# Attention in a hybrid DeltaNet block: the low-part products of the value step issued apart from the high-part products

## The chip, the core and the metric

The kernel runs on one core of one Trainium2 chip. The metric is the device time of the whole program in microseconds (us). The core has five engines that run side by side, each through its own list of instructions in order: TensorE (PE in the profile, with its weight loads as PEld), VectorE (DVE), ScalarE (ACT), GpSimd (POOL) and SyncE (SP), which issues the transfers.

## What is computed

One layer of a streaming encoder on 2048 tokens of 1024 channels. The normalised input goes through one wide projection; that feeds a gated delta rule (4 heads of 128) and a stick-breaking attention (8 heads of 64); both results are gated, projected, merged and added to the input. The part that matters here is the attention:

```python
def _stick_breaking(q, k, v):
    ...
    for blk in range(s // SB_BLOCK):
        ...
        z = jnp.einsum('bhqd,bhkd->bhqk', q[:, :, q0:end], k[:, :, :end]) * scale
        ...
        log_keep = jnp.where(mask, jax.nn.log_sigmoid(-z), 0.0)
        rest = lax.cumsum(log_keep, axis=3, reverse=True) - log_keep
        a = jnp.where(mask, jnp.exp(jax.nn.log_sigmoid(z) + rest), 0.0)
        outs.append(jnp.einsum('bhqk,bhkd->bhqd', a, v[:, :, :end]))
```

The weights `a` times the values `v` is the step that the change touches. All is in float32. The kernel splits both factors of a large product into a high part, rounded to the format `F32R`, and a low part (the rest), and adds up the products of the parts.

## The kernel before

The program has four stretches. First the projections for the delta rule and for q, k, v, with the triangular solves beside them. Then attention, in the gaps of the projections for the output gates. Then the delta rule's state recurrence, one chunk of 128 tokens after the other, in the gaps of the last gate blocks and of the up projections (`up`, results named y). Last the output projection (`outs`, results named o).

A gate block (`mm_chan`, L384) is eight groups of three 512-column products into one PSUM bank (named pj): high by high, high by low, low by high. Behind each group `gap` (L273) is called. It adds `third` = 1.1 x 3 x 512 / 2400 = 0.704 us of credit (L232), and `advance` (L156) lets the generator `attention` (L958) issue pieces until the credit, which is kept up to 4.0, is used up or the generator has nothing that may go (it yields None). A piece costs what `self.clock` advanced meanwhile. That clock is the planner's own: `mm` (L121) adds columns / 2400 us for each F32R product, at least 256 columns, and `tr` (L126) 128 / 1200 us for each transpose. So a pj group is 0.64 us on it. The order that comes out on TensorE is fixed by `pin` (L130), each product behind the one before. The order on the other engines is left to the scheduler of the framework.

Attention goes over four groups of 512 queries, the 8 heads, and blocks of 512 keys from the diagonal backwards. For each of four tiles of 128 queries `att_tile` (L1053) makes the scores z (two products), two sigmoids on ACT, the mask on the diagonal and the scan on DVE (L1069), a copy of the carry (L1072), and the weights s on POOL (L1073). For every pair of tiles and every 256 keys (a part m; a pair has two, the first pair on the diagonal one) there are two more steps. `tr` (L1013) calls `att_trans` (L1076): four transposes (three on an edge) into the PSUM tile `at`, the high part `hi` cast by ACT (L1088), the low part `lo` = at - hi by DVE (L1089). `pv` (L1018) calls `att_av` (L1092): for both blocks of 128 keys the values `vt` as weights, and `hi` and then `lo` as the 256 moving columns, added up in the PSUM tile `av`. In the diagonal's edge parts the second block has 128 columns. There are 288 parts, so 576 products with hi and 576 with lo.

Two lists hold the steps until the clock reaches their due time: `trans`, LT = 4.5 us behind the pair's second tile, and `prods`, LP = 2.2 us behind the transposes. `ready` (L965) takes the head of `prods` if it is due, otherwise the head of `trans` if it is due and `prods` has fewer than two entries. A new tile starts at the earliest 1.3 us (LZ) after the one before, and with fewer than NS = 6 weight tiles alive; the transposes of a pair free its two. `at`, `hi` and `lo` have two buffers each, `av` one. The first pv of a head calls `att_begin`, the last `att_end` (ACT copies half of av, DVE adds, POOL multiplies by the gate).

When attention is over, `gap` turns to the delta rule (`dn_states`), which first waits 9.0 us of the planner's clock for its loads. The projection list has 17 units (3 of zb, 14 of gates) of 32 groups in which attention may run, and the last two gate blocks (64 groups) come behind them; were attention not over by then, the rest of it would be issued alone (`drain`, L176).

Of the kernel before, what the change touches and what calls it, by code (L numbers as in the profile page):

```python
# [18 lines left out]
P = 128  # L19
# [18 lines left out]
class Block:  # L38
# [914 lines left out]
        nc.gpsimd.affine_select(self.future, self.future, pattern=[[1, P]], compare_op=ALU.is_ge, fill=0.0, base=0, channel_multiplier=-1)  # L953


    LT, LP, LZ = 4.5, 2.2, 1.3

    def attention(self):  # L958

        nc, ap = self.nc, self.ap  # L960
        trans, prods = [], []
        live = {"s": 0, "v": 0}
        first = [0.0]

        def ready():  # L965

            if prods and prods[0][0] <= self.clock:
                prods.pop(0)[1]()
            elif trans and trans[0][0] <= self.clock and len(prods) < 2:
                trans.pop(0)[1]()  # L970
            else:
                return False
            return True

        for qg in (2, 0, 1, 3):
            qs = slice(qg * TG, qg * TG + TG)
            for h in range(SH):
                hs = slice(SD * h, SD * h + SD)
                qt = ap.tile([P, 2, TG], F32R, tag="qt", name="qt", bufs=2)
                for dup in range(2):  # L980
                    nc.sync.dma_start(qt[SD * dup:SD * dup + SD].bitcast(F32), self.d_q[:, hs, qs].rearrange("n p t -> p n t"))
                carry = [None] * 4
                for kc in range(qg, -1, -1):
                    while live["v"] >= 3:
                        yield 0.0 if ready() else None
                    live["v"] += 1
                    kt = ap.tile([P, TG], F32R, tag="kt", name="kt", bufs=2)
                    vt = ap.tile([P, 4, P], F32R, tag="vt", name="vt", bufs=3)
                    for part in range(2):
                        nc.sync.dma_start(kt[SD * part:SD * part + SD].bitcast(F32), self.d_k[part, hs, kc * TG:kc * TG + TG])  # L990
                    nc.sync.dma_start(vt.bitcast(F32), self.d_v[h, :, 4 * kc:4 * kc + 4])
                    diag = kc == qg
                    A = []
                    for i in range(4):
                        while True:
                            if ready():
                                yield 0.0
                            elif self.clock >= first[0] and live["s"] < self.NS:
                                break
                            else:  # L1000
                                yield None
                        w = P * (i + 1) if diag else TG
                        first[0] = self.clock + self.LZ * (w + P) / (TG + P)
                        live["s"] += 1
                        A.append(self.att_tile(qt, kt, i, w, diag, carry))
                        if i % 2:
                            n = 1 if diag and i == 1 else 2
                            for m in range(n):
                                edge = diag and 2 * m == i - 1
                                begin = diag and i == 1  # L1010
                                end = kc == 0 and i == 3 and m == n - 1

                                def tr(A=A[i - 1:i + 1], vt=vt, m=m, i=i, kc=kc, h=h, qs=qs, edge=edge, begin=begin, end=end, done=m == n - 1, vdone=i == 3 and m == n - 1):  # L1013
                                    parts = self.att_trans(A, m, edge)
                                    if done:
                                        live["s"] -= 2

                                    def pv():  # L1018
                                        if begin:
                                            assert self.zb_done > h // 2  # L1020
                                            self.att_begin(h, qs)
                                        self.att_av(self.av[:, (i - 1) * P:(i + 1) * P], vt, parts, m, edge, begin, end)
                                        if vdone:
                                            live["v"] -= 1
                                        if end:
                                            self.att_end(h, qs)
                                    prods.append((self.clock + self.LP, pv))
                                trans.append((self.clock + self.LT, tr))
                        yield 0.0
        while trans or prods:  # L1030
            yield 0.0 if ready() else None
        self.attended = True
# [56 lines left out]
        nc.vector.tensor_tensor(lo[:, c:], flat[:, c:], hi[:, c:].bitcast(F32), ALU.subtract)  # L1089
        return hi, lo  # L1090

    def att_av(self, av, vt, parts, m, edge, first, last):  # L1092
        for k in range(2):
            c = P if edge and k == 1 else 0
            for n, b in enumerate(parts):
                b = b[:, (1 - k) * 2 * P:(2 - k) * 2 * P]
                self.mm(av[:, c:], vt[:, 2 * m + k], b[:, c:], start=first and k == 0 and n == 0, stop=last and k == 1 and n == 1)


_INS = ["x", "norm_gain", "w_in", "b_gate", "conv_w", "a_log", "dt_bias", "dn_out_gain", "sb_q_gain", "sb_k_gain", "w_up_a", "w_up_b", "w_out"]  # L1100
# [21 lines left out]
```

## Time and profile before

| | |
|---|---|
| median of 3 runs | 2099.04 us (2095.98 to 2099.79) |
| the profiled execution's own time | 2102.16 us |
| its span, first to last instruction | 2100.5 us |
| PE busy | 2045.1 us, 97% |
| PEld busy | 1822.8 us, 87% |
| DVE busy | 1360.8 us, 65% |
| POOL busy | 935.3 us, 45% |
| ACT busy | 909.3 us, 43% |
| mean granted TensorE clock | 0.996 |
| attention (first z to last av product) | 770 to 1543 us |

The profile is one execution. A row of a listing names the line, the engine, the operation, what is written and what is read (`av<-hi,vt` is a product with the moving operand hi and the weights vt into av), the shape and the count, then busy time, mean duration and the idle time of the engine just before such instructions with what ended it. In a listing in order of time each row begins with the start and the length in us, and brackets hold the idle time ahead of it. Matmuls overlap each other in these rows, so the distance of two starts says more of what one costs than its length.

### The profile page before, as it was taken

Reading aid. Unit: us, or ns where it says so; the run is one execution under the profiler, and the core shown is the slowest. Engines: PE = TensorE matmul, PEld = TensorE weight load, DVE = VectorE, ACT = ScalarE, POOL = GpSimd, SP = SyncE. Lnnn points to the kernel's source line nnn. Section 1 sums busy time; section 2 is a strip of 40 time slices with the busy share of each in tenths; the row PEclk is TensorE's granted clock in tenths of the full one; section 3 lists DMA queues with packets and bytes.
Section 4 is the critical chain, followed back from the end, with each engine's and each line's share of the span. In section 5 each row is a group of like instructions: output and inputs, shape, how many; then the busy total and the mean of one; then the engine's idle time right before and its main releaser. Section 6 shows DMA issues by size and latency. Waiting matters only on the chain.

```text
span 2100.5 us, 36701 instructions
## 1 busy us (share of the span) xinstructions
PE 2045.1 (97%) x12903; PEld 1822.8 (87%) x12903; DVE 1360.8 (65%) x2547; ACT 909.3 (43%) x1919; POOL 935.3 (45%) x1140
## 2 busy tenths in 40 slices
PE   7999999999999999999999999999999899999999
PEld 7987887789999988888878888888888799999887
DVE  7356777768998238787887877877744466433221
ACT  6335655322222136666666666666633321211110
POOL 4346777433342225455555555555437545521000
PEclk9999999999999999999999999999999999999999
DMA  7213333226334543333664544333347786754442
GB/s 238 66 61 101 111 116 101 81 75 132 106 111 127 150 126 107 111 110 112 176 161 131 137 110 114 103 112 110 86 142 235 246 237 211 235 183 141 147 141 81
DMA packets 279703, 282.53 MB, mean 135 GB/s; under 512 B 49440, under 2 KB 215520, under 8 KB 279392
## 3 DMA queue, kind: packets, MB, share of 16 engines
q1 hardware_dynamic: 279520, 280.19, 44.9%
q8 instruction: 103, 1.69, 0.3%
q14 instruction: 80, 0.66, 0.1%
HBM read 177.35 MB, written 102.76 MB: 133 GB/s over the span
## 4 chain that ended last, share of the span: by engine, by line
PE 38%; DVE 4%; DMA 4%; ACT 2%; issue 2%; POOL 1%; SPq 1%; DVEq 0%; ACTq 0%; POOLq 0%
PE pj L124 10%; PE o L124 8%; PE y L124 7%; PE dn L124 4%; PE av L124 3%; PE at L128 3%; PE z L124 3%; DVE r L1069 2%; DMA wraw<-in_w_in_dram 2%; DVE lo L1089 1%; DMA ot<-d_ob 1%; ACT z L1067 1%; ACT s L1066 1%; DMA raw<-in_w_out_dram 1%; DMA gt<-d_g 0%
## 5 line engine op out<-in xcount | busy, mean ns | idle before, releaser
L1073 POOL TENSOR_TENSOR s<-s,r 128x512 f32<-128x512 f32 (+2 forms) x320 | 306.3, 958 | 334.7 <-DVE r L1069 327.5
L124 PE MATMUL pj<-xh,whi 128*128 128x512 f32 x1024 | 419.5, 410 | 1.9 <-DVE one L948 1.9
L124 PE MATMUL pj<-xh,wlo 128*128 128x512 f32 x1024 | 405.3, 396 | 0.0
L124 PE MATMUL pj<-xl,whi 128*128 128x512 f32 x1024 | 404.6, 395 | 0.0
L124 PE MATMUL pj<-whi,xh 128*128 128x256 f32 (+1 forms) x1024 | 293.0, 286 | 1.2 <-ACT xh L380 1.2
L124 PE MATMUL pj<-wlo,xh 128*128 128x256 f32 (+1 forms) x1024 | 289.3, 283 | 0.2 <-DVE wlo L330 0.2
L124 PE MATMUL pj<-whi,xl 128*128 128x256 f32 (+1 forms) x1024 | 289.4, 283 | 0.0
L1069 DVE TENSOR_TENSOR_SCAN r<-z,carry,zero 128x512 f32<-128x512 f32 x192 | 245.7, 1280 | 64.4 <-ACT z L1067 59.8
L124 PEld LDWEIGHTS pj<-xh,wlo 128*128 128x128 f32 x1024 | 192.7, 188 | 44.4
L1066 ACT ACTIVATE s<-z 128x512 f32<-128x512 f32 (+2 forms) x320 | 171.7, 536 | 133.1 <-PE z L124 54.2
L124 PEld LDWEIGHTS pj<-xh,whi 128*128 128x128 f32 x1024 | 193.4, 189 | 33.6 <-issue 2.1
L124 PEld LDWEIGHTS pj<-xl,whi 128*128 128x128 f32 x1024 | 193.8, 189 | 32.1
L1089 DVE TENSOR_TENSOR lo<-at,hi 128x512 fp32r<-128x512 f32 (+1 forms) x288 | 182.6, 650 | 26.9 <-ACT hi L1088 25.6
L124 PEld LDWEIGHTS pj<-whi,xh 128*128 128x128 f32 x1024 | 193.9, 189 | 1.6 <-ACT xh L380 1.6
L124 PEld LDWEIGHTS pj<-wlo,xh 128*128 128x128 f32 x1024 | 194.1, 190 | 0.5 <-DVE wlo L330 0.5
L124 PEld LDWEIGHTS pj<-whi,xl 128*128 128x128 f32 x1024 | 193.7, 189 | 0.3 <-DVE xl L381 0.3
L1088 ACT CAST hi<-at 128x512 fp32r<-128x512 f32 (+1 forms) x288 | 154.2, 567 | 84.8 <-PE at L128 82.4
L124 PE MATMUL z<-kt,qt 128*128 128x512 f32 (+3 forms) x640 | 188.7, 376 | 0.6 <-DVE r L1069 0.5
L330 POOL TENSOR_TENSOR wlo<-wraw,whi 128x512 fp32r<-128x512 f32 (+2 forms) x66 | 115.3, 1746 | 130.9 <-ACT whi L329 114.8
L1067 ACT ACTIVATE z<-z 128x512 f32<-128x512 f32 (+2 forms) x320 | 170.8, 534 | 0.0
L128 PE MATMUL at<-ident,s 128*128 128x128 f32 x1088 | 155.6, 274 | 1.6 <-POOL s L1073 1.2
L124 PE MATMUL av<-lo,vt 128*128 128x256 f32 x576 | 147.3, 290 | 9.2 <-DVE lo L1089 4.3
(199 smaller groups left out, 4300.7 us busy)
## 6 DMA issues: line engine op xcount, KB each, us to landing
kt<-d_k SPq DMA_DIRECT2D x160, 128.0 KB, 3.0
vt<-d_v SPq DMA_DIRECT2D x80, 256.0 KB, 3.4
xt<-in_x_dram SPq DMA_DIRECT2D x32, 512.0 KB, 3.6
qt<-d_q SPq DMA_DIRECT2D x64, 256.0 KB, 5.2
d_g<-sg SPq DMA_DIRECT2D x128, 128.0 KB, 2.4
gt<-d_g SPq DMA_DIRECT2D x64, 256.0 KB, 3.3
wraw<-in_w_in_dram SPq DMA_DIRECT2D x56, 256.0 KB, 3.5
wraw<-in_w_in_dram SPq DMA_DIRECT2D x18, 512.0 KB, 4.1
```

Of the source, the lines that this page charges most:

```text
L124: self.pin(self.nc.tensor.matmul(out, lhsT, rhs, **kw))
L128: self.pin(self.nc.tensor.transpose(*args))
L330: (eng or nc.gpsimd).tensor_tensor(lo[:, ks, :n], raw[:, :, :n], hi[:, ks, :n].bitcast(F32), ALU.subtract)
L1066: nc.scalar.activation(s[:, :w], z[:, :w], AF.Sigmoid, scale=SD ** -0.5)
L1067: nc.scalar.activation(z[:, :w], z[:, :w], AF.Sigmoid, scale=-(SD ** -0.5))
L1069: nc.vector.tensor_tensor_scan(r[:, 0:w][:, ::-1], z[:, 0:w][:, ::-1], self.zero.to_broadcast([P, w]), init, ALU.mult, ALU.add)
L1073: nc.gpsimd.tensor_mul(s[:, :w], s[:, :w], r[:, 1:w + 1])
L1088: nc.scalar.copy(hi[:, c:], flat[:, c:])
L1089: nc.vector.tensor_tensor(lo[:, c:], flat[:, c:], hi[:, c:].bitcast(F32), ALU.subtract)
```

## The change

The four products of a part are parted. `pv` issues the two products with `hi` (for both blocks of keys), and puts a new step `rest` at the head of `prods`, due LL = 0.4 us of the planner's clock later. `rest` issues the two products with `lo`, and then does what stood at the end of `pv`: it counts down the live value tiles and calls `att_end` at a head's end. As `rest` stands in `prods`, it counts against the limit of two, and nothing behind it in the list goes before it; a new tile may, and so may the transposes while `rest` is the only entry. The products, the tiles, the buffers and the other engines' instructions are the same.

```diff
-    LT, LP, LZ = 4.5, 2.2, 1.3
+    LT, LP, LL, LZ = 4.5, 2.2, 0.4, 1.3
...
                                         if begin:
                                             assert self.zb_done > h // 2
                                             self.att_begin(h, qs)
-                                        self.att_av(self.av[:, (i - 1) * P:(i + 1) * P], vt, parts, m, edge, begin, end)
+                                        self.att_av(self.av[:, (i - 1) * P:(i + 1) * P], vt, parts[0], m, edge, start=begin)
+                                        prods.insert(0, (self.clock + self.LL, rest))
+
+                                    def rest():
+                                        self.att_av(self.av[:, (i - 1) * P:(i + 1) * P], vt, parts[1], m, edge, stop=end)
                                         if vdone:
                                             live["v"] -= 1
                                         if end:
...
-    def att_av(self, av, vt, parts, m, edge, first, last):
+    def att_av(self, av, vt, b, m, edge, start=False, stop=False):
         for k in range(2):
             c = P if edge and k == 1 else 0
-            for n, b in enumerate(parts):
-                b = b[:, (1 - k) * 2 * P:(2 - k) * 2 * P]
-                self.mm(av[:, c:], vt[:, 2 * m + k], b[:, c:], start=first and k == 0 and n == 0, stop=last and k == 1 and n == 1)
+            self.mm(av[:, c:], vt[:, 2 * m + k], b[:, (1 - k) * 2 * P + c:(2 - k) * 2 * P], start=start and k == 0, stop=stop and k == 1)
```

## Rows read from the trace of the kernel before

**Rows 1.** attention's stretch: length, busy us (instructions) of PE, PEld, DVE, ACT, POOL, clock

```profile
770.00:1543.00 773.00, 757.16 (x4420) 649.74 (x4419) 612.67 (x1100) 520.53 (x1058) 406.79 (x687) 1.00 0.42 117
```

**Rows 2.** groups on PE in attention: busy us, mean ns | idle before, releasers

```profile
L124 PE MATMUL pj<-xh,whi 128*128 128x512 f32 x512 | 211.2, 413 | 0.0
L128 PE MATMUL at<-ident,s 128*128 128x128 f32 x1088 | 155.6, 274 | 1.6 <-POOL s L1073 1.2 <-DVE lo L1089 0.3
L124 PE MATMUL av<-lo,vt 128*128 128x256 f32 x512 | 136.2, 292 | 9.2 <-DVE lo L1089 4.3 <-DVE carry L1072 4.0
L124 PE MATMUL av<-hi,vt 128*128 128x256 f32 x512 | 135.4, 288 | 4.4 <-ACT hi L1088 4.1 <-issue 0.3
```

**Rows 3.** waits of PE's weight loads: us in total, times, longest us

```profile
PEld av L124 <- DVE lo L1089: 11.3, 22, 1.4
PEld av L124 <- DVE carry L1072: 6.7, 12, 1.3
PEld av L124 <- ACT hi L1088: 6.3, 8, 2.0
PEld at L128 <- POOL s L1073: 6.2, 14, 0.8
PEld z L124 <- DVE r L1069: 2.3, 4, 0.7
```

**Rows 4.** PE in order of time where nothing waits, with products and transposes

```profile
1533.25 0.28 PE L124 MATMUL av<-hi,vt 128*128 128x256 f32 x1
1533.37 0.28 PE L124 MATMUL av<-lo,vt 128*128 128x256 f32 x1
1533.49 0.28 PE L124 MATMUL av<-hi,vt 128*128 128x256 f32 x1
...
1534.21 0.39 PE L124 MATMUL pj<-xh,whi 128*128 128x512 f32 x1
1534.44 0.40 PE L124 MATMUL pj<-xl,whi 128*128 128x512 f32 x1
...
1534.91 1.03 PE L128 MATMUL at<-ident,s 128*128 128x128 f32 x8
1535.70 0.48 PE L124 MATMUL pj<-xh,whi 128*128 128x512 f32 x1
```

**Rows 5.** PE in order of time around the longest wait for a low part

```profile
1098.81 0.28 PE L124 MATMUL av<-hi,vt 128*128 128x256 f32 x1
1100.22 0.39 PE L124 MATMUL av<-lo,vt 128*128 128x256 f32 x1 [1.13 <-DVE carry L1072]
1100.44 0.23 PE L124 MATMUL av<-hi,vt 128*128 128x128 f32 x1
1100.50 0.27 PE L124 MATMUL av<-lo,vt 128*128 128x128 f32 x1
1100.62 0.62 PE L128 MATMUL at<-ident,s 128*128 128x128 f32 x4
```

**Rows 6.** DVE in order of time in the same stretch

```profile
1098.44 1.28 DVE L1069 TENSOR_TENSOR_SCAN r<-z,carry,zero 128x512 f32<-128x512 f32 x1
1099.63 0.53 DVE L1089 TENSOR_TENSOR lo<-at,hi 128x384 fp32r<-128x384 f32 x1
```

**Rows 7.** groups of weight loads of the value products in attention

```profile
L124 PEld LDWEIGHTS av<-hi,vt 128*128 128x128 f32 x576 | 108.7, 189 | 13.8 <-ACT hi L1088 6.3 <-issue 0.7
L124 PEld LDWEIGHTS av<-lo,vt 128*128 128x128 f32 x576 | 108.6, 189 | 24.7 <-DVE lo L1089 11.3 <-DVE carry L1072 6.7
```

**Rows 8.** PE in order of time: first and last of four late products

```profile
780.85 0.39 PE L124 MATMUL av<-lo,vt 128*128 128x256 f32 x1 [0.60 <-DVE lo L1089]
...
1124.09 0.39 PE L124 MATMUL av<-lo,vt 128*128 128x256 f32 x1 [1.07 <-DVE carry L1072]
```

**Rows 9.** groups on PE behind attention: projection products that are left

```profile
L124 PE MATMUL pj<-xh,whi 128*128 128x512 f32 x95 | 40.7, 428 | 0.0
```

**Rows 10.** PE in order of time: first product of the delta rule

```profile
1553.59 1.95 PE L124 MATMUL dn<-state,kq 128*128 128x128 f32 x16
```

## Prediction

> **What bounds the kernel now.** I read the engine shares first, then the table of busy time by stretch. TensorE (PE) is busy 97% of the span. Attention [rows 1] runs from 770 to 1543 us: PE is busy 757.16 of 773.00 us there, the granted clock is 1.00, and DVE, the next engine, is busy 612.67 us (79%). So the stage ends when PE's own list ends, and PE loses time only where an instruction at the head of its list waits. The grouped listing of PE [rows 2] says where: 9.2 us before the products of the low parts (av<-lo), 4.4 us before those of the high parts (av<-hi), 1.6 us before the transposes (at) and nothing before the projection products (pj). The reader is to see that the one step which the change moves holds over half of PE's idle time in this stage.
>
> That listing understates a stall, because a matmul's modelled end covers the beginning of the wait behind it. The waits of PE's weight loads begin earlier [rows 3]: 11.3 us (22 times) for `lo` of L1089 and 6.7 us (12 times) put down to the carry copy that DVE runs right behind `lo`, together **18.0 us in 34 waits**. The order of time bears this out: where nothing waits, a 256-column product starts 0.12 us after the one before it [rows 4]; of the 576 starts of av<-lo, 34 came more than 0.1 us later than that, 15.8 us in all, and the product behind such a start came another 0.1 us late (0.22 us instead of 0.12), 3.4 us. 15.8 + 3.4 = 19.2 us against 18.0 us; I go on with 18.0. The largest case [rows 5]: hi product at 1098.81, lo product at 1100.22, 1.41 us instead of 0.12. The DVE rows of the same stretch [rows 6] give the cause: DVE begins a scan of 1.28 us at 1098.44 and only then, at 1099.63, `lo`. So PE stands behind the second half of the split, not behind the first.
>
> **The change, part by part.**
>
> *What stays.* The products are the same, 576 with hi and 576 with lo, each with its own weight load [rows 7]. No DMA, no copy and no instruction of another engine is added. In the old order hi and lo follow each other on the same 128x128 block of values, in the new order they don't. In [rows 4] the starts hi to lo (same block) and lo to hi (other block) are both 0.11 to 0.12 us apart, so the pairing saves nothing now and the parting costs nothing. The Trainium skill, "TensorE: Matmul & The Clock Gate", section "Step-by-step: what each phase is for", speaks against the change here: weights can stay put across several matmuls, so that one load serves many. The trace disagrees for this kernel, with 1152 loads for 1152 products. By the Trainium skill's figure on the same page for a load of 128 columns (section "LDWEIGHTS (loading the stationary operand)", 128/1.2, some 107 ns) 576 saved loads that were now lost would be worth an estimated 61 us; by the trace it is nothing.
>
> *Where 128-column products lie.* In the 64 diagonal parts the second product has 128 columns, in the order hi256, lo256, hi128, lo128; now it is hi256, hi128, and later lo256, lo128. The two short ones start 0.06 us apart and the next instruction 0.12 us behind the second [rows 5]: what follows a pair of them is late by a load. Parted, each may pay that by itself: bounds 0 and 64 x 0.06 = 4 us; a gain is excluded, since the short products are no longer back to back anywhere. Transposes, 128 columns too, take 0.10 us each in a row of eight [rows 4], as much as the pair's mean with its follower, so a load is paid for each short product already: I take 0.
>
> *What moves.* After the hi products (0.24 us) the planner puts the lo products at the head of its list, due 0.4 us of its clock later. What fills that time is a group of three pj products (0.70 us, 0.23 each [rows 4]; 0.64 on the planner's clock), a score tile, or, for the second part of a pair, the transposes of the next pair, whose list is free by then (four, 0.4 us). All this is work that PE has to do anyway. A lo wait of 0.70 us or less then disappears. Of the 34, four were larger: 0.85, 1.15, 1.29 and 1.26 us late (the third in [rows 5], the first and the last in [rows 8], where the idle time shown is some 0.2 us shorter); 0.15 + 0.45 + 0.59 + 0.56 = 1.8 us stay. If only a score tile of 0.46 us or four transposes stand between, the same list leaves 4 us. So the direct gain is 18.0 - 2 to 4 = 14 to 16 us.
>
> *What may come back.* DVE still does its 612.67 us of work in the stage. No wait is added by the code; the wait on `lo` stands later. Queued behind a late `lo` product are the second part's hi products, the next transposes, and with them ACT's cast and DVE's next `lo`. How much new waiting the later place brings isn't shown before; the bounds are 0 and all 18. The nearest row is the other PE step that the planner holds back until its input should be there, the transposes: 272 to 288 such steps lose 6.2 us in 14 waits [rows 3]. I let the lo step lose as much as that, 6 us in place of 18, residual included. **Gain 12 us.** The 6.3 us for hi [rows 3] stay: hi keeps its due time.
>
> *The hold on the planner's loop.* While the lo step waits at the head, the second part and, where two are listed, the next transposes can't go. By the planner's own prices (0.43 us for a part's transposes and also for its four products) the loop transposes, 2.2 us, products, transposes took at least 0.43 + 2.2 + 0.43 + 0.43 = 3.49 us for a pair, and now 3.49 - 0.21 + 0.64 = 3.9 us (the last lo may follow the next transposes). What a pair gets is set by the credit: attention costs 358 us by these prices (z 119, av 123, at 116), the 512 pj groups inside it [rows 2] give 0.704 each, 360 us; (358 + 512 x 0.64) / 144 pairs = 4.8 us. 4.8 is above 3.9, so the credit still sets the pace and attention takes the same number of groups, give or take two. After it 95 pj groups are left [rows 9], 64 of which are the last two gate blocks; 31 are to spare. The 16 groups from 1542.69 to 1553.59 that cover the first loads of the delta rule [rows 9, 10] stay covered.
>
> *The sum.* The stages before 770 us are untouched, and those after 1543 us do the same work, so what attention gains arrives at the end. The profiled execution took 2102.16 us (span 2100.5); less 12 is 2090.2. It lies 3.1 us above the median of the runs shown, 2099.04, so the forecast for the median is 2099.0 - 12 = **2087 us**.
>
> **The rivals.**
>
> *A. The stall only moves (no change).* DVE is what PE waits for, and a PE that no longer stops asks DVE for the next `lo` and the next scan sooner. For: in the rows around the largest stall DVE goes from a scan of 1.28 us straight to `lo` [rows 6]. Against: DVE is idle a fifth of the stage [rows 1], and all other PE waits on DVE and POOL together (z, at) are 8.5 us [rows 3], so there is room ahead of those steps. All 18 us return: 2099 us. Also here: the lo step comes due so soon that little stands between, or attention takes a few groups more and the delta rule loses cover that it had.
>
> *B. The hold slows the loop and attention overruns its cover (slower).* It decides at 4.8 + 31 x 0.64 / 144 = 4.9 us per pair. One group of hold gives 3.9 us; if the credit is used up when the lo step comes due, a second group passes, 4.55 us, and the rounding to whole groups at two other due times (half a group each, 0.3 us) brings it to 4.9 to 5.2. At 5.2 us, 144 x 0.4 / 0.64 = 90 groups more are wanted, 59 beyond the 31; at 3.6 groups a pair some 16 pairs run with nothing beside them, each idle for about the 2.2 us between transposes and products, 35 us, and the 10.9 us ahead of the delta rule lie open. 2099 - 12 + 35 + 11 = 2133 us. Against: credit is kept up to 4 us, so that a late group is made up for by a burst, and bursts of 8 av and 8 at products without pj between them are in the trace.
>
> *C. The loads (slower).* If two products on one block shared a load now, parting them would add 576 loads, at the 0.10 us of a load-bound transpose [rows 4] 58 us: 2099 - 12 + 58 = 2145 us. The count of loads [rows 7] speaks against it. This is the Trainium skill's rule from the page and section named above.
>
> **How the numbers follow.** Forecast (a gain of 5 to 22 us) 0.68; rival A 0.20; rival B 0.10; rival C 0.02. The upper end takes in A with the scatter of the runs (2095.98 to 2099.79), 2101; B and C and a little of A are left out, 0.12 to 0.14. The lower end: all lo stalls gone, and half of the hi waits with them because the casts spread out, 2099 - 18 - 3 = 2078. A run can tell 0.2%, 4.2 us, from no change: faster 0.68, same 0.20, slower 0.12.
>
> **What would show it.** Right: the waits of PE and of its loads for `lo` fall from 18 us to 6 or less; in the order of time three pj products, a score tile or transposes stand between two hi and two lo products; attention ends near 1531 us on the profile's span, with about 95 pj groups left, and the length of what follows is unchanged within 3 us. Wrong: waits of the same size before at, z or av<-hi (A); fewer than 64 pj groups after attention's end, or PE idle beside bare av and at groups (B); loads of av above 1152 or longer starts (C).

## The result, and the profile after

The changed kernel takes 2115.31 us (median of 4 runs, 2112.75 to 2117.58) against 2097.51 us for the kernel before in 4 runs: **slower, by a factor of 1.0076 (95% interval 1.0063 to 1.0089; the two medians alone give 1.0085)**. The forecast was 2087 us, in a range of 2078 to 2101. The profiled execution took 2113.18 us.

The page of the changed kernel, span and PE:

```profile
span 2111.3 us, 36719 instructions
PE 2041.2 (97%) x12903; PEld 1824.2 (86%) x12903; DVE 1366.3 (65%) x2547; ACT 913.1 (43%) x1919; POOL 933.9 (44%) x1140
```

PE's work is the same (12903 products and transposes, as before), its share is the same, and the span is 10.8 us longer. The stretch of attention (length, busy us of PE, PEld, DVE, ACT and POOL, granted clock), which answers to [rows 1], now ends at 1558 us in place of 1543:

```profile
770.00:1558.00 788.00, 755.00 (x4419) 652.81 (x4418) 613.33 (x1098) 524.03 (x1053) 404.53 (x686) 0.99 0.41 115
```

PE is idle 33 us of it, before 16 us of 773 [rows 1]. The groups of the weight loads of the value products and two waits of the weight loads, which answer to [rows 3, 7]:

```profile
L124 PEld LDWEIGHTS av<-hi,vt 128*128 128x128 f32 x576 | 97.9, 188 | 53.6 <-DVE ot L1051 25.9 <-DVE carry L1077 9.7 <-ACT hi L1093 4.7
L124 PEld LDWEIGHTS av<-lo,vt 128*128 128x128 f32 x576 | 103.5, 189 | 22.0 <-DVE carry L1077 2.5 <-DVE lo L1094 0.2
PEld at L128 <- POOL s L1078: 3.5, 5, 1.3
PEld z L124 <- DVE r L1074: 0.6, 2, 0.4
```

The reader is to see that the wait named in the forecast is gone, and that another is there. Ahead of the low products 18.0 us have become 2.7 (0.2 put down to `lo`, 2.5 to the carry copy behind it). Ahead of the **high** products stand 25.9 us put down to `ot` of L1051, which did not occur before, and 9.7 us put down to the carry copy that follows it on DVE: 35.6 us (the 38 us in the expectations below count the 2.5 us of the carry copy ahead of the low products as well). `ot` is the sum with which `att_end` takes a head's result out of the PSUM bank of av. There is one such bank, and the first product of the next head writes it.

One of these hand-offs in order of time. Changed kernel, PE (start, length, what, idle time ahead):

```profile
860.72 0.49 PE L128 MATMUL at<-ident,s 128*128 128x128 f32 x3
860.97 0.48 PE L124 MATMUL av<-hi,vt 128*128 128x256 f32 x2
...
862.45 0.40 PE L124 MATMUL av<-lo,vt 128*128 128x256 f32 x2
...
863.38 0.62 PE L124 MATMUL z<-kt,qt 128*128 128x512 f32 x2
866.19 0.45 PE L124 MATMUL av<-hi,vt 128*128 128x256 f32 x2 [2.19 <-DVE carry L1077]
```

Next ACT's copy out of av, then DVE, in the same stretch:

```profile
864.22 0.58 ACT L1050 COPY tmp<-av 64x512 f32<-64x512 f32 x1
864.28 1.28 DVE L1074 TENSOR_TENSOR_SCAN r<-z,one,zero 128x512 f32<-128x512 f32 x1 [1.21 <-ACT z L1072]
865.48 0.66 DVE L1051 TENSOR_TENSOR ot<-av,tmp 64x512 f32<-64x512 f32 x1
```

The same hand-off in the kernel before, PE and DVE's sum:

```profile
862.17 0.28 PE L124 MATMUL av<-lo,vt 128*128 128x256 f32 x1
862.29 0.49 PE L128 MATMUL at<-ident,s 128*128 128x128 f32 x3
...
865.82 0.37 PE L124 MATMUL av<-hi,vt 128*128 128x256 f32 x1
```

```profile
864.34 0.68 DVE L1046 TENSOR_TENSOR ot<-av,tmp 64x512 f32<-64x512 f32 x1
```

Before, a head's last low product (862.17) was followed by the next part's transposes (862.29), and from these the planner counts its 2.2 us to the next head's first product, which came at 865.82. DVE's sum had ended at 865.02. Now the transposes (860.72) stand ahead of the last part's high products (860.97), the low products follow a score tile and a pj group later (862.45), and ACT's copy and DVE's sum can only come behind them, the sum behind a scan of 1.28 us. The next head's first product is due while all that is still to come, and waits 2.19 us until 866.19.

More often the transposes of the next head slip in between a head's last high products and its last low ones. Such a hand-off of the changed kernel on PE:

```profile
800.21 0.39 PE L124 MATMUL av<-hi,vt 128*128 128x256 f32 x2
800.44 0.49 PE L128 MATMUL at<-ident,s 128*128 128x128 f32 x3
...
801.22 0.40 PE L124 MATMUL av<-lo,vt 128*128 128x256 f32 x2
...
805.28 0.45 PE L124 MATMUL av<-hi,vt 128*128 128x256 f32 x2 [1.84 <-DVE carry L1077]
```

Over the 31 hand-offs, in the mean and counted from the start of a head's last product: the sum ended 2.80 us behind it before and 2.95 us in the changed kernel, so emptying the bank takes about as long as it did. But the next product started 0.73 us behind the sum's end before (3 of 31 within 0.13 us of it), and 0.13 us now (26 of 31). The place of the transposes that belong to the next head's first part tells why. Before, they came behind the last low product in 28 of 31 hand-offs; in the changed kernel they do so in 3, in 22 they stand between the last high and the last low products, and in 6 ahead of the high ones. All 35.6 us stand in these 28, none in the other 3.

A second loss lies behind some of the waits. The stretch behind the wait above, in windows of 2 us (the granted clock is the third number from the end):

```profile
864.00:866.00 2.00, 0.00 (x1) 0.00 (x0) 1.72 (x2) 1.86 (x4) 0.29 (x1) 1.00 0.65 195
866.00:868.00 2.00, 1.81 (x9) 1.61 (x10) 1.54 (x4) 0.80 (x2) 1.39 (x3) 0.91 0.00 0
868.00:870.00 2.00, 2.00 (x6) 1.54 (x6) 1.07 (x2) 1.40 (x3) 1.99 (x3) 0.50 0.07 26
870.00:872.00 2.00, 2.00 (x12) 1.67 (x11) 1.06 (x2) 0.49 (x2) 0.95 (x1) 0.74 0.63 180
872.00:874.00 2.00, 2.00 (x11) 1.60 (x10) 1.58 (x3) 2.00 (x5) 0.27 (x2) 1.00 0.20 61
```

Behind the wait the granted clock goes to 0.50, the lower of its two levels (1.2 GHz), and comes back. Summed over the windows (2 us times what is missing to 1.00) this dip costs 1.7 us. In attention the kernel before has one dip, behind its longest wait for `hi` (PE idle for 1.76 us until 1019.64); the changed one has four, one behind a wait for `hi` (1.95 us) and three behind hand-offs (1.84, 2.19 and 2.12 us), so 5.1 us of the loss are the clock's. Not every wait of that length is followed by one: in e2 below 4 of 14 waits over 1.7 us are not.

### The profile page after: what moved, and what is told of

Read it like the earlier page. It is cut to its first block, busy times and chain, and to the rows that moved or that the text cites. A ratio compares the mean times of both kernels' runs of the same rounds, so it can differ in the third digit from the quotient of the medians.

```text
span 2111.3 us, 36719 instructions
## 1 busy us (share of the span) xinstructions
PE 2041.2 (97%) x12903; PEld 1824.2 (86%) x12903; DVE 1366.3 (65%) x2547; ACT 913.1 (43%) x1919; POOL 933.9 (44%) x1140
## 4 chain that ended last, share of the span: by engine, by line
PE 63%; DVE 13%; ACT 5%; DMA 5%; issue 4%; POOL 2%; SPq 1%; DVEq 0%; ACTq 0%; POOLq 0%
PE pj L124 31%; PE o L124 8%; PE y L124 7%; DVE r L1074 5%; PE av L124 4%; PE at L128 4%; PE z L124 3%; PE dn L124 3%; DVE acc L548 2%; DMA wraw<-in_w_in_dram 2%; ACT z L1072 2%; DVE lo L1094 1%; PE tp L128 1%; ACT s L1071 1%; DMA raw<-in_w_out_dram 1%
## 5 line engine op out<-in xcount | busy, mean ns | idle before, releaser
L1093 ACT CAST hi<-at 128x512 fp32r<-128x512 f32 (+1 forms) x288 | 158.5, 566 | 82.8 <-PE at L128 77.2
L128 PE MATMUL at<-ident,s 128*128 128x128 f32 x1088 | 165.8, 276 | 1.9 <-POOL s L1078 1.7
L889 ACT CAST xh<-ot 128x256 fp32r<-128x256 f32 x128 | 50.2, 406 | 235.9 <-PE o L124 99.1
```

Of the source, the lines that this page charges most:

```text
L128: self.pin(self.nc.tensor.transpose(*args))
L889: nc.scalar.copy(hi, t)
L1093: nc.scalar.copy(hi[:, c:], flat[:, c:])
```

## The experiments

Each is compared with runs of the kernel before on the same chip (ratio with its 95% interval; the medians of before were 2099.8 beside e1 to e4, 2098.9 beside e5 to e8 and 2102.1 beside e9 and e10). "Hand-off" is what stands before the high products and is put down to the emptying of av or to the carry copy behind the sum; "lo" what stands before the low products; both are waits of the weight loads in the one profiled execution, and the dips are those in attention.

| kernel | median us | ratio to before | hand-off us | lo us | clock dips |
|---|---|---|---|---|---|
| before | 2097.5 | | 0 | 18.0 | 1 |
| changed | 2115.3 | 1.0063 to 1.0089 | 35.6 | 2.7 | 4 |
| e1, ends together | 2085.5 | 0.9911 to 0.9941 | 7.0 | 3.7 | 1 |
| e2, ends alone apart | 2142.9 | 1.0197 to 1.0229 | 40.5 | 6.3 | 10 |
| e3, no overtaking | 2099.0 | 0.9985 to 1.0012 | 17.4 | 2.9 | 3 |
| e4, hold 0 | 2098.5 | 0.9984 to 1.0002 | 0 | 11.6 | 1 |
| e5, emptied by ACT | 2099.4 | 0.9983 to 1.0006 | 20.2 | 3.4 | 1 |
| e6, first product later | 2100.5 | 0.9996 to 1.0014 | 11.3 | 4.1 | 2 |
| e7, e1 and emptied by ACT | 2089.8 | 0.9943 to 0.9968 | 7.2 | 5.0 | 1 |
| e8, before, emptied by ACT | 2107.2 | 1.0022 to 1.0041 | 7.6 | 15.2 | 1 |
| e9, two banks for av | 2111.1 | 1.0030 to 1.0063 | 0 | 1.6 | 4 |
| e10, control to e9 | 2136.1 | 1.0145 to 1.0186 | 30.0 | 0.4 | 1 |

**e1: at a head's end the low products follow at once.**

```diff
-                                        prods.insert(0, (self.clock + self.LL, rest))
+                                        if end:
+                                            rest()
+                                        else:
+                                            prods.insert(0, (self.clock + self.LL, rest))
```

> Changed kernel, but at a head's last part the low products follow the high ones at once; the other 256 parts stay apart. Theory T (the loss is the hand-off of the one bank of av from head to head: at a head's end the next head's transposes, which start the 2.2 us to its first product, now go ahead of the last low products, and the first product waits for DVE's sum out of av, 25.9 + 12.2 = 38 us in 28 waits of the changed kernel): these waits fall to 5 us or less, those for lo come back only at the 32 ends, 2 us; 2084 to 2093 us, faster than before. Rival R1 (holding back the low parts slows the loop everywhere): nothing much changes, 2108 to 2116 us.

2085.45 us, 0.9926 of before. The loads of the value products, and the hand-off of above in order of time:

```profile
L124 PEld LDWEIGHTS av<-hi,vt 128*128 128x128 f32 x576 | 99.1, 189 | 26.4 <-DVE ot L1054 4.2 <-ACT hi L1096 3.8 <-DVE carry L1080 2.8
L124 PEld LDWEIGHTS av<-lo,vt 128*128 128x128 f32 x576 | 103.0, 189 | 22.8 <-DVE carry L1080 2.8 <-DVE lo L1097 0.9
```

```profile
861.09 0.40 PE L124 MATMUL av<-hi,vt 128*128 128x256 f32 x2
861.32 0.40 PE L124 MATMUL av<-lo,vt 128*128 128x256 f32 x2
861.56 0.49 PE L128 MATMUL at<-ident,s 128*128 128x128 f32 x3
...
864.82 0.34 PE L124 MATMUL av<-hi,vt 128*128 128x256 f32 x2
```

The last low products (861.32) stand directly behind the high ones, the transposes behind them, and the next head's first product (864.82) waits for nothing. 256 parts are still apart, and the wait for `lo` has stayed away. So the held low parts of these 256 gain what was forecast, and the 32 ends lost all of it and more, some 30 us. This kernel beats both.

The hand-off fell to 7.0 us, not to 5 or less as expected. The next head's transposes go ahead even of the last *high* products in 8 hand-offs, and all 7.0 us stand in 5 of these. The longest:

```profile
1060.43 0.49 PE L128 MATMUL at<-ident,s 128*128 128x128 f32 x3
...
1061.68 0.34 PE L124 MATMUL av<-hi,vt 128*128 128x256 f32 x2
1061.99 0.45 PE L124 MATMUL av<-lo,vt 128*128 128x256 f32 x2
...
1066.50 0.45 PE L124 MATMUL av<-hi,vt 128*128 128x256 f32 x2 [2.31 <-DVE carry L1080]
```

**e2: the kernel before, with only the head ends apart.** The last part of a head is issued as in the changed kernel, all others hi, lo, hi, lo:

```diff
+                                        if not end:
+                                            self.att_both(self.av[:, (i - 1) * P:(i + 1) * P], vt, parts, m, edge, begin)
+                                            if vdone:
+                                                live["v"] -= 1
+                                            return
```

> Kernel before, with the low products held back at the 32 head ends alone; the other 256 parts are issued hi, lo, hi, lo as before. T: the hand-off waits of the changed kernel are there (25 to 40 us in some 28 waits) and the lo waits of before too (16 to 18 us): 2115 to 2135 us. R1: 32 of 288 holds, a ninth of the loss of 18 us: 2098 to 2101 us.

2142.88 us, 2.1% slower than before and more than was expected.

```profile
L124 PEld LDWEIGHTS av<-hi,vt 128*128 128x128 f32 x576 | 108.2, 192 | 54.8 <-DVE carry L1082 22.0 <-DVE ot L1056 18.5 <-ACT hi L1098 7.9
L124 PEld LDWEIGHTS av<-lo,vt 128*128 128x128 f32 x576 | 110.2, 192 | 15.6 <-DVE carry L1082 3.9 <-DVE lo L1099 2.4
```

40.5 us of hand-off (22.0 + 18.5) from 32 parts alone: the rival that every held part slows the loop is out. Ten clock dips take another 17 us, nine of them new, 15 us. One thing was missed: the wait for `lo` should have stayed at 16 to 18 us and fell to 6.3. I take it that DVE catches up while PE waits at the hand-offs; no run tells that apart.

**e3: no transposes while a head's last low products are held back.** `ready` gets one more condition:

```diff
-            elif trans and trans[0][0] <= self.clock and len(prods) < 2:
+            elif trans and trans[0][0] <= self.clock and len(prods) < 2 and not first[1]:
```

(`first[1]` is true from a head's last high products to its last low ones.)

> Changed kernel, all 288 parts apart, but while a head's last low products are held back no transposes are issued. T, if the overtaking is the cause and not the hold of 0.4 us itself: the first product of the next head again comes 3 us or more behind the last low products, hand-off waits at most 8 us, 2085 to 2096 us. If the hold itself is the cause, the waits stay at 25 us or more: 2105 to 2115 us.

2099.04 us, no different from before, between the two expectations.

```profile
L124 PEld LDWEIGHTS av<-hi,vt 128*128 128x128 f32 x576 | 98.1, 189 | 39.4 <-DVE ot L1053 11.7 <-DVE carry L1079 5.7 <-ACT hi L1095 5.5
L124 PEld LDWEIGHTS av<-lo,vt 128*128 128x128 f32 x576 | 105.8, 189 | 24.9 <-DVE lo L1096 1.9 <-DVE carry L1079 1.0
```

Hand-off 17.4 us, half of the changed kernel's. In 11 of the 31 hand-offs the next head's transposes had been issued ahead of the last part's *high* products, as at 860.72 above, which this condition doesn't stop, and all 17.4 us stand in these 11. In the other 20 the transposes come behind the last low products, and there no product waits for the emptying, though the low products are held back there too, 0.75 us in the mean. So it is the overtaking that makes the wait, and the hold only by letting it happen; the hand-off stayed above the 8 us expected because the condition stops only that part of the overtaking which happens behind the high products.

**e4: the hold set to 0** (`LL` 0.0 in place of 0.4).

> Changed kernel with the hold at 0 in place of 0.4 us: hi, hi, lo, lo right behind each other in nearly every part, as many products on the same block no longer neighbours as in the changed kernel. T: no hand-off waits over 5 us, lo waits of 12 to 20 us as before, 2094 to 2102 us. Rival R2 (two products on one block of values share something that parting them loses): starts of av products over 0.13 us apart where nothing waits, and 2115 us or more.

2098.52 us, no different from before.

```profile
L124 PEld LDWEIGHTS av<-hi,vt 128*128 128x128 f32 x576 | 99.1, 188 | 20.5 <-ACT hi L1093 6.8 <-issue 0.9
L124 PEld LDWEIGHTS av<-lo,vt 128*128 128x128 f32 x576 | 89.6, 189 | 14.7 <-DVE lo L1094 6.2 <-DVE carry L1077 5.4
```

With hi, hi, lo, lo behind each other no hand-off waits, and most of the `lo` wait is there again, 11.6 us, a third less than before and just under what was expected. That two products on one block of values are no longer neighbours costs nothing that the time shows.

**e5: av emptied by two copies of ACT, the sum on POOL from SBUF**, so that DVE's queue is out of the hand-off:

```diff
-        nc.vector.tensor_tensor(ot[a:a + SD], av[a:a + SD], tmp[a:a + SD], ALU.add)
+        nc.scalar.copy(ot[a:a + SD], av[a:a + SD])
+        nc.gpsimd.tensor_tensor(ot[a:a + SD], ot[a:a + SD], tmp[a:a + SD], ALU.add)
```

> Changed kernel, all parts apart, but av is emptied at a head's end by two copies of ACT (0.58 us each) and summed from SBUF on POOL, so that the next head no longer waits for DVE's queue. In the changed kernel the sum ended 3.1 us after the last low product was issued (1.0 to the copy, 1.4 from there to the sum, 0.7 the sum). T: with two copies it is some 2.2 us, each of the 26 waiting hand-offs gets 0.9 us back, 23 us: 2088 to 2098 us. If not the hand-off but the held low parts cost the time, it stays at 2110 us or more.

2099.39 us, 16 us better than the changed kernel and just above what was expected.

```profile
L124 PEld LDWEIGHTS av<-hi,vt 128*128 128x128 f32 x576 | 98.2, 188 | 36.2 <-ACT ot L1051 20.2 <-ACT hi L1094 3.5
```

The same wait is now put down to ACT's second copy, and has shrunk from 35.6 to 20.2 us: a faster emptying takes a part of the loss away, with the order unchanged. Some 5 of the 16 us are the three clock dips that went with the waits.

**e6: a head's first product due 1.6 us later.**

```diff
-                                    prods.append((self.clock + self.LP, pv))
+                                    prods.append((self.clock + self.LP + (1.6 if begin else 0.0), pv))
```

> Changed kernel, all parts apart, but a head's first product comes due 1.6 us of the planner's clock later (3.8 in place of 2.2 us behind its transposes). T: the waits for the hand-off, 38 us in 28, 1.4 us each, fall below 10 us as TensorE gets other work in front: 2084 to 2097 us. If the bank itself were the bound and not the place in the order, the wait would go elsewhere: 2108 us or more.

2100.53 us, outside both expectations. The hand-off fell to 11.3 us, but not below 10.

```profile
L124 PEld LDWEIGHTS av<-hi,vt 128*128 128x128 f32 x576 | 97.6, 189 | 36.1 <-ACT hi L1093 12.1 <-DVE carry L1077 5.9 <-DVE ot L1051 5.4
```

The hand-off shrinks with other work in front of it, as the theory has it; but the wait for `hi` rises from 4.7 to 12.1 us, so that the gain over before doesn't come. Why the casts are late there was not tried.

**e7 and e8: the emptying by ACT of e5 in e1, and in the kernel before.**

> Head ends together as in e1_end_together, and av emptied by two copies of ACT. T: of the 9.7 us of hand-off waits left there 5 us or more go: 2077 to 2085 us. If ACT's extra 32 copies delay its casts (ACT is busy two thirds of attention), as much comes back: 2084 to 2089 us.

> Kernel before with av emptied by two copies of ACT. T: no product waits for the hand-off there (the sum ends 0.7 us ahead of the next product in the mean), so nothing is to be had: 2095 to 2102 us. If the way of emptying av is better by itself, 2092 us or less.

2089.76 us and 2107.24 us: neither is what was expected of the theory, and in both the way of e5 makes a kernel slower, by 0.3%, whose hand-off was all or mostly in order. High products of e7, then of e8:

```profile
L124 PEld LDWEIGHTS av<-hi,vt 128*128 128x128 f32 x576 | 99.1, 189 | 27.8 <-ACT ot L1054 7.2 <-ACT hi L1097 7.2
```

```profile
L124 PEld LDWEIGHTS av<-hi,vt 128*128 128x128 f32 x576 | 108.5, 188 | 20.2 <-ACT ot L1046 7.6 <-ACT hi L1089 6.2
```

In e8 7.6 us of waiting for ACT's second copy are new. In e7 the hand-off is as long as in e1 (7.2 and 7.0 us), and the wait for `hi` is 7.2 in place of 3.8 us. So e5's gain doesn't come from a better way to empty av; it shortens a chain that the change had made critical.

**e9 and e10: two banks for av, taken from z, and the control.** e9 has `pz` with two buffers in place of three and `pv` with two in place of one, e10 only the first of it, both on the changed kernel.

> Changed kernel, all parts apart, with two PSUM banks for av; the bank is taken from the scores z (two in place of three). T (a head's first product waits only because the one bank of av is not empty): no waits for the hand-off at all, below 3 us; against the same kernel with one bank for av (e10_z2_av1) 25 to 40 us faster, whatever the lost bank of z costs. If the wait had another cause, the two differ by less than 10 us.

> Control to e9_z2_av2: changed kernel with two banks for z and one for av. T: the hand-off waits of the changed kernel, 25 to 40 us, and more waits of the score tiles for a bank of z; 2115 to 2150 us.

2111.14 and 2136.05 us: the second bank of av is worth 24.9 us, just under what was expected. High products and score products, e9, then e10:

```profile
L124 PEld LDWEIGHTS av<-hi,vt 128*128 128x128 f32 x576 | 100.5, 190 | 17.4 <-ACT hi L1093 3.9
L124 PEld LDWEIGHTS z<-kt,qt 128*128 128x128 f32 x640 | 106.6, 190 | 49.6 <-DVE r L1074 38.1
```

```profile
L124 PEld LDWEIGHTS av<-hi,vt 128*128 128x128 f32 x576 | 98.8, 189 | 46.6 <-DVE ot L1051 25.3 <-DVE carry L1077 4.7 <-ACT hi L1093 4.5
L124 PEld LDWEIGHTS z<-kt,qt 128*128 128x128 f32 x640 | 105.7, 189 | 47.7 <-DVE r L1074 36.7
```

With two banks the hand-off wait is gone, with one it is 30.0 us; the other waits are alike, only three more clock dips, 5.1 us, count against e9. The next head's transposes go ahead of the last low products in 28 of 31 hand-offs in both, so the overtaking costs only where the bank is not free. That settles that the product waits for the bank. As the second bank is taken from z, it is paid for with 38 us of waiting for scans, and the pair is no way out.

## Why the prediction was wrong

*What bounds the kernel, and what the low parts cost:* right. The wait for `lo` was 18.0 us, and the hold removes it: 2.7 us are left in the changed kernel and 3.7 in e1, less than the 6 that I had let it keep by the transposes' row. A gain of about 12 us is what e1 shows: attention ends there at 1532 us in place of 1543, 11 us sooner, and another 4 us of its 15 lie behind attention. It is in part luck, since 7.0 us of hand-off, which the sum did not have, stand against 2.3 us less of `lo` than it allowed and 2.5 us less of waiting for `hi`.

*What stays:* right. The loads are 1152 as before, and e4 puts the pairing at nothing, so rival C is out. The 128-column products cost nothing, as taken. By the distances of starts (medians), the two short ones took 0.22 us together before and 0.11 each in the changed kernel where pj products follow; where transposes follow, it is 0.20 us together and 0.08 each, so that the gain which the text excludes exists, but is under 2 us in all.

*The hold on the loop:* right. Behind attention 92 pj groups are left in the changed kernel, 95 before [rows 9], three groups for 288 holds where I had said "give or take two"; rival B is out.

```profile
L124 PE MATMUL pj<-xh,whi 128*128 128x512 f32 x92 | 39.3, 428 | 0.0
```

*What may come back:* **this is the step that failed.** It says that no wait is added by the code, and lists behind the low product only what is queued on PE and the casts that follow. But the step that was moved, `rest`, issues more than two products. At a head's end it also issues `att_end`: ACT's copy, DVE's sum, and with them the release of the one bank of av, on which the next head's first product waits. That wait was in the code before as well, and cost nothing, since the sum ended 0.73 us ahead of it in the mean. The change takes away more than this: as `rest` leaves the list of transposes free, the 2.2 us to the next head's first product begin to run ahead of it, 1.0 us ahead of the last low product in the mean of 22 hand-offs and 1.8 us in 6, where before they began behind the last product in 28 of 31. e3 shows that this is what counts, as the hold without the overtaking brought no wait. The bounds of 0 and 18 us held only waits of the same kind; the new one was 35.6 us.

*The rivals:* A says that the stall moves, prices it at no more than the stall removed, and looks for it at z, at and av<-hi. It did turn up at av<-hi, at twice the price and by another mechanism, the hand-off of a bank between heads. No rival named it, though the text on the kernel told that av has one buffer and that `att_end` is called at the last product.

*The sum:* in the waits of the loads 35.6 us of hand-off were added and 15.3 us of `lo` removed, and the others fell, by 1.6 us for `hi`, 1.7 for z and 2.7 for the transposes [rows 3]. With 5.1 us of clock that is 19 us, where the span grew by 10.8. PE's own idle time lies nearer, since a load's wait begins earlier than PE is idle (PE itself waits 18.6 + 7.5 us for the hand-off): it grew by 17.2 us, from 15.8 to 33.0, in a stretch that is 15 us longer. The stages behind attention are 4.3 us shorter (553.6 against 557.9 us): three pj groups of 0.70 us moved ahead into attention, and the dips of the granted clock cost 1.7 us less there. Some 6 us between the waits of the loads and the length of attention stay open.

## What to carry to other kernels

Where a step is moved back, list all that it issues or releases and not only the instructions that give it its name: the last product of an accumulation also carries the emptying of its bank, and with one bank the next accumulation waits for that. List also what may now overtake it: here the transposes that start the next head's count. A wait that costs nothing in the trace has a slack that can be read, here 0.73 us between the sum's end and the next product; an overtaking by 1 us turned it into a stall. Defer the parts in the middle, and let the last one go at once. The Trainium skill, "Trainium Kernel Development and Optimization", section "Best Practices", says that "consistent bubbles can mean SBUF/PSUM ran out"; here they came at 26 of 31 changes of head, and e9 against e10 bears it out with 24.9 us for one bank.

## What the runs showed of the hardware

A wait of TensorE can cost more than its length. In attention the granted clock fell to 0.50 behind some waits, and each such dip took 1.7 us more: four in the changed kernel (waits of 1.84 to 2.19 us), ten in e2 (1.81 to 3.34 us), one in e1 (2.31 us). And the emptying of a bank is long for its work: the copy takes 0.58 us and the sum 0.68 us, but from the start of the last product to the sum's end it was 2.8 us in the kernel before, with 0.76 us ahead of the copy and 0.77 us between the copy and the sum. In the hand-off at 862.45 above it is a scan of 1.28 us on DVE that the sum stands behind.
